# Value products of an encoder trunk: three matmuls of 256 columns replaced by one of 512 and one of 256

## Chip, cores and metric

The kernel runs on one core of a Trainium2 chip. The metric is the device time of one execution in microseconds (us), lower is better. Three runs of the kernel before took 2064.1, 2063.9 and 2063.29 us.

## What is computed

The reference is a trunk of two layers on 256 tokens of width 2048, all in float32. Each layer is a normalization, a projection to queries, keys and values, attention of 16 heads of width 128, an output projection with a residual, and an MLP of width 8192 with a squared ReLU. The part that the change touches is the projection to values.

```python
proj = h @ w_in                                            # layer 0: q, k, v of 16 heads
qa, ka, va, qb, kb, vb = jnp.split(proj, [...], axis=-1)
oa = neighbourhood_attention(split_heads(qa, 8), split_heads(ka, 8), split_heads(va, 8), rpb)
ob = dilated_attention(split_heads(qb, 8), split_heads(kb, 8), split_heads(vb, 8))
x = x + jnp.concatenate([merge_heads(oa), merge_heads(ob)], axis=-1) @ w_out
...
proj = h @ w_qkv                                           # layer 1: q of 16 heads, k and v of 4
q, k, v = jnp.split(proj, [wq, wq + wkv], axis=-1)
o = banded_attention(split_heads(q, 16), split_heads(k, 4), split_heads(v, 4), 128, 1, slopes, sink=sink)
x = x + merge_heads(o) @ w_out
...
x = x + sq_relu_mlp(rms_norm(x, g), w1, w2)                # after either attention
```

## The kernel before

**Precision.** A float32 product is made of three products of a rounded type (fp32r). Every operand is split in a high part (a copy in that type) and a low part (what the copy lost): `split` does it with one instruction on ACT (the high part, L86) and one on DVE (the low part, L87). The product is then high·high + high·low + low·high.

**Units.** A unit is a block of 128 columns of a weight matrix with all 2048 rows: 16 tiles of 128x128, which come in two halves of 8 tiles (512 KB each) by a DMA that SP issues. `load_halves` gives a half a raw buffer, a buffer for its high parts (`whi`, five of them) and one for its low parts (`wlo`, five). `k_range` multiplies: for each of 16 `k` there is a matmul of 512 columns (L160: the weight's high part is stationary, the activation's high and low parts lie side by side in `u` and move), and one of 256 columns (L162: the weight's low part by the activation's high part). The first fills a whole PSUM bank `acc` of 512 columns, the second adds to its first half. `joined` then copies the second half of the bank to SBUF on ACT (L189, tile `t`) and adds the first half to it on DVE (L191, tile `z`). There are three `acc` banks.

**Values.** The values of two heads (256 columns of weights) are needed with tokens on the partitions, so here the activation is stationary and the weights move. `value_products` (L281) does for each `k` and each half `j` of the tokens three matmuls of 256 columns: activation high by weight high, high by low, and low by high. All add to the same 256 columns of one bank, in which `j` = 0 and `j` = 1 lie side by side. There are 10 such pairs of heads: the first is in the start stage (L467 on, 16 packs that hold a slice of the input and of the first weights), seven more are in layer 0, two in layer 1. That is 10 x 16 x 2 x 3 = 960 matmuls. `keep_values` then reads the bank: ACT writes the high part `v` with the token's scale (L301), DVE the low part (L302).

**Order.** The code is written as one stream of units with steps that fall due after so many `tick`s (one per four `k` of a unit, or per two `k` of a value pair); a scheduler then orders each engine's instructions by what it expects to be ready. So where a step falls on an engine is not to be read from the code alone. Around the end of a value pair in layer 0 there stand: the first matmuls of the next unit, the transposes `p_ps` of the pair's second head (L342), and the products `m_ps` of the weights of attention with the values of the pair's first head (L361), which need `v`. Each `v` tile is read by six such matmuls a head: `v` high of `j` = 0 twice, then `v` low of `j` = 0, then the same for `j` = 1. Other names in the rows: `s_ps` are scores (L317), `st` and `s` the softmax, `pt` the transposed attention weights, `ssq` sums of squares, `rcol` the scale of a token, `toep` and `tabs` tables for the biases, `hid` the hidden part of the MLP, `o` the heads' outputs. L481 and L482 are the start stage's own products for the first two heads' queries and keys.

## Time and profile before

| | |
|---|---|
| median of three runs | 2063.9 us (2063.29 to 2064.1) |
| the profiled execution | 2064.23 us |
| its span, first to last instruction | 2062.3 us |
| granted TensorE clock, mean | 0.996 |
| PE busy (matmuls) | 2042.2 us, 99% |
| DVE busy, ACT busy | 1340.3 us (65%), 1036.9 us (50%) |
| instructions on PE | 12438 matmuls, 12438 loads of weights |

PE is the engine of the matmuls, PEld its loads of stationary operands, which run beside them. A matmul's own duration in the rows is from its start to its end with the pipeline's fill, so that durations overlap: a matmul of 512 columns shows 390 ns where the next one starts 227 ns later. What counts is the distance from one start to the next.

### The profile page before, as it was taken

The page shows a single profiled execution, that of the slowest core. Times are in us where ns is not written, and L with a number is a line of the kernel's source. Part 1 is how long each engine was busy: PE and PEld are TensorE (multiplying, and loading weights), DVE is VectorE, ACT ScalarE, POOL GpSimd, SP SyncE. Part 2 cuts the span into 40 slices and gives each one's busy share as a digit, 9 for nine tenths or more (in the row PEclk, how much of TensorE's full clock was granted, in tenths as well). Part 3 has the DMA queues.
Part 4 walks back from the last instruction along what each step waited for, and adds up shares of the span by engine and source line. Part 5 has one row for each costly group of instructions (what it writes and reads, how often), then busy time and mean ns, then how long its engine had stood idle before and what let it go on. Part 6 is the DMA issues. An engine that isn't in the chain of part 4 may idle for free.

```text
span 2062.3 us, 31803 instructions
## 1 busy us (share of the span) xinstructions
PE 2042.2 (99%) x12438; PEld 1825.3 (89%) x12438; DVE 1340.3 (65%) x2083; ACT 1036.9 (50%) x1597; POOL 18.5 (1%) x26
## 2 busy tenths in 40 slices
PE   8999999999999999999999999999999999999997
PEld 7999998888888888888889998888888888888886
DVE  7766666766655556666666877766665556665554
ACT  6555555554544444444445655654444444444442
POOL 2100000000000000000000000000000000000000
PEclk9999999999999999999999999999999999999998
DMA  8655555555555555555555444555555555555552
GB/s 311 204 174 168 175 169 184 195 186 193 194 194 194 193 194 195 194 194 194 194 194 185 154 155 152 189 188 193 195 193 192 194 195 193 193 193 194 193 193 92
DMA packets 107174, 388.16 MB, mean 188 GB/s; under 512 B 12128, under 2 KB 12400, under 8 KB 107024
## 3 DMA queue, kind: packets, MB, share of 16 engines
q1 hardware_dynamic: 106128, 383.83, 55.9%
q0 software_dynamic: 752, 2.27, 0.3%
q8 instruction: 97, 1.59, 0.3%
q14 instruction: 53, 0.43, 0.1%
q10 hardware_dynamic: 144, 0.04, 0.0%
HBM read 383.99 MB, written 2.10 MB: 187 GB/s over the span
## 4 chain that ended last, share of the span: by engine, by line
PE 98%; DVE 1%; DMA 0%; ACT 0%; issue 0%; POOL 0%; DVEq 0%; POOLq 0%
PE acc L160 58%; PE acc L162 30%; PE acc L281 5%; PE s_ps L317 1%; PE m_ps L361 1%; PE p_ps L342 1%; DMA tabs<-in_tabs 0%; PE s_ps L481 0%; PE acc L481 0%; ACT h L86 0%; DVE l L87 0%; DVE xs L581 0%; PE acc L482 0%; PE acc L158 0%; PE acc L157 0%
## 5 line engine op out<-in xcount | busy, mean ns | idle before, releaser
L87 DVE TENSOR_TENSOR l<-r,h 128x1024 fp32r<-128x1024 f32 (+1 forms) x724 | 881.3, 1217 | 654.2 <-ACT h L86 652.5
L86 ACT ACTIVATE h<-r 128x1024 fp32r<-128x1024 f32 (+1 forms) x724 | 762.4, 1053 | 915.5 <-PE acc L160 604.0
L160 PE MATMUL acc<-u,h 128*128 128x512 f32 x2804 | 960.5, 390 | 0.3 <-DVE z L191 0.3
L162 PE MATMUL acc<-u,l 128*128 128x256 f32 x2804 | 774.5, 276 | 0.0
L160 PE MATMUL acc<-hid,h 128*128 128x512 f32 x2016 | 685.6, 389 | 0.0
L160 PEld LDWEIGHTS acc<-u,h 128*128 128x128 f32 x2804 | 526.5, 188 | 107.1 <-DVE z L191 0.4
L162 PE MATMUL acc<-hid,l 128*128 128x256 f32 x2048 | 565.5, 276 | 0.0
L162 PEld LDWEIGHTS acc<-u,l 128*128 128x128 f32 x2804 | 526.5, 188 | 0.1
L160 PEld LDWEIGHTS acc<-hid,h 128*128 128x128 f32 x2016 | 378.4, 188 | 78.5
L162 PEld LDWEIGHTS acc<-hid,l 128*128 128x128 f32 x2048 | 384.5, 188 | 0.0
L160 PE MATMUL acc<-o,h 128*128 128x512 f32 x500 | 173.2, 392 | 1.2 <-DVE z L191 1.2
L162 PE MATMUL acc<-o,l 128*128 128x256 f32 x500 | 139.0, 278 | 0.0
L281 PE MATMUL acc<-h,u 128*128 128x256 f32 x640 | 122.2, 283 | 0.0
L191 DVE TENSOR_TENSOR z<-acc,t 128x256 f32<-128x256 f32 x273 | 113.6, 418 | 2.1 <-ACT t L189 2.1
L160 PEld LDWEIGHTS acc<-o,h 128*128 128x128 f32 x500 | 93.9, 188 | 21.9 <-DVE z L191 1.9
L281 PEld LDWEIGHTS acc<-h,u 128*128 128x128 f32 x640 | 101.7, 189 | 1.0
L189 ACT ACTIVATE t<-acc 128x256 f32<-128x256 f32 x273 | 100.2, 368 | 4.3 <-PE acc L162 2.3
L162 PEld LDWEIGHTS acc<-o,l 128*128 128x128 f32 x500 | 93.9, 188 | 0.0
L281 PE MATMUL acc<-l,u 128*128 128x256 f32 x320 | 90.3, 282 | 0.0
L281 PEld LDWEIGHTS acc<-l,u 128*128 128x128 f32 x320 | 60.6, 189 | 0.0
L403 DVE SCALAR_TENSOR_TENSOR z<-z 128x256 f32<-128x256 f32 x128 | 54.3, 425 | 4.2
L86 ACT ACTIVATE hid<-z 128x256 fp32r<-128x256 f32 x128 | 51.3, 402 | 6.0 <-DVE z L403 6.0
(105 smaller groups left out, 869.8 us busy)
## 6 DMA issues: line engine op xcount, KB each, us to landing
r<-in_w_mlp_in SPq DMA_DIRECT2D x256, 512.0 KB, 3.5
r<-in_w_mlp_out SPq DMA_DIRECT2D x256, 512.0 KB, 3.6
r<-in_even_w_in SPq DMA_DIRECT2D x56, 512.0 KB, 3.6
r<-in_odd_w_qkv SPq DMA_DIRECT2D x40, 512.0 KB, 3.5
r<-in_even_w_out SPq DMA_DIRECT2D x32, 512.0 KB, 3.5
r<-in_odd_w_out SPq DMA_DIRECT2D x32, 512.0 KB, 3.6
r<-in_even_w_v SPq DMA_DIRECT2D x28, 512.0 KB, 3.5
r<-in_start SPq DMA_DIRECT2D x16, 512.0 KB, 4.7
```

What stands on the lines that cost most here:

```text
L86: nc.scalar.activation(hi, src, AF.Copy)
L87: nc.vector.tensor_sub(lo, src, hi.bitcast(F32))
L160: nc.tensor.matmul(ps, h, act[:, k].rearrange("p a t -> p (a t)"), start=start, stop=False)
L162: nc.tensor.matmul(ps[:, :T], l, act[:, k, 0, :], start=False, stop=stop)
L189: nc.scalar.activation(t, ps[:, T:], AF.Copy)
L191: nc.vector.tensor_add(z, ps[:, :T], t)
L281: nc.tensor.matmul(out, u[:, k, x, js], y, start=k == 0 and j == 0 and n == 0, stop=k == KT - 1 and n == 2, skip_group_check=True)
L317: nc.tensor.matmul(s_ps[:, i, :], qh[:, x, qs], kh[:, y, :], start=n == 0, stop=n == 2)
L342: nc.tensor.transpose(p_ps[:, j, i * P:(i + 1) * P], s[:, i, j * P:(j + 1) * P], ident)
L361: nc.tensor.matmul(o_ps[:, :T], vv[:, x, j, side * P:(side + 1) * P], pt[:, y, j, :], start=n == 0, stop=n == 5)
L403: nc.vector.scalar_tensor_tensor(z, z, 0.0, z, op0=ALU.max, op1=ALU.mult)
```

## The change

The value products get the form of the other units. For each `k` and `j` there is one matmul of 512 columns (activation high by the weights' low and high parts side by side) and one of 256 (activation low by the weights' high part), which adds to the second half. Each `j` has a bank of its own, which is joined (ACT, DVE) before `keep_values` splits it: in the pairs after the first these are two of the three `acc` banks, in the start stage one `acc` and one `m_ps` bank. High and low parts of a half now lie in one buffer (five of 2112 columns, in place of five of 1024 and five of 1088), and for the values the low part stands first. In the start stage the weights of a pack, split in one step of 768 columns before, are split in two steps of 512 and 256.

```diff
+STEP = 16
+PART_SIZE = 2 * HALF * P + 4 * STEP
...
-    whi = ctx.enter_context(tc.tile_pool(name="whi", bufs=PART_BUFS))
-    wlo = ctx.enter_context(tc.tile_pool(name="wlo", bufs=PART_BUFS))
+    parts_w = ctx.enter_context(tc.tile_pool(name="parts_w", bufs=PART_BUFS))
...
+    def value_rows(w, n):
+        at = n * P + STEP
+        return w[:, STEP:STEP + 2 * at].rearrange("p (a c) -> p a c", c=at)[:, :, :n * P] \
+                .rearrange("p a (k c) -> p a k c", c=T)
...
             if flat:
-                h, l = (w.rearrange("p k c -> p (k c)") for w in (h, l))
-                split(h, l, r.rearrange("p k c -> p (k c)"))
-                loaded.append((h, l, None))
+                w = value_rows(w, HALF)
+                split(w[:, 1], w[:, 0], r.rearrange("p (k a) c -> p k (a c)", a=2))
+                loaded.append((w, None, None))
...
-    def value_products(ps, k, h, l):
+    def value_products(ps, k, w):
         for j in range(2):
             js = slice(j * P, (j + 1) * P)
-            out = ps[:, j * T:(j + 1) * T].rearrange("p (a c) -> p a c", a=2)
-            for n, (x, y) in enumerate(((0, h), (0, l), (1, h))):
-                nc.tensor.matmul(out, u[:, k, x, js], y, start=k == 0 and j == 0 and n == 0,
-                                 stop=k == KT - 1 and n == 2, skip_group_check=True)
+            nc.tensor.matmul(ps[j].rearrange("p (a t) -> p a t", a=2), u[:, k, 0, js], w, start=k == 0, stop=False)
+            nc.tensor.matmul(ps[j][:, T:], u[:, k, 1, js], w[:, 1, :], start=False, stop=k == KT - 1)
 
     def value_pair(pool, keep):
-        ps = acc_ps.tile([P, 2 * T], F32, name="acc")
+        ps = [acc_ps.tile([P, 2 * T], F32, name="acc") for _ in range(2)]
...
     def keep_values(pool, keep, ps):
-        ps = ps.rearrange("p (a t) -> p a t", a=2)
         w = pool.tile([P, 2, 2, T], F32R, name="v", bufs=1)
         for j in range(2):
-            nc.scalar.activation(w[:, 0, j, :], ps[:, j, :], AF.Copy, scale=rcol[:, j:j + 1])
-            nc.vector.scalar_tensor_tensor(w[:, 1, j, :], ps[:, j, :], rcol[:, j:j + 1],
+            z = joined(ps[j])
+            nc.scalar.activation(w[:, 0, j, :], z, AF.Copy, scale=rcol[:, j:j + 1])
+            nc.vector.scalar_tensor_tensor(w[:, 1, j, :], z, rcol[:, j:j + 1],
                                            w[:, 0, j, :].bitcast(F32), op0=ALU.mult, op1=ALU.subtract)
...
-    vps = acc_ps.tile([P, 2 * T], F32, name="acc")
+    vps = acc_ps.tile([P, 2 * T], F32, name="acc"), aux_ps.tile([P, 512], F32, name="m_ps", bufs=2)
...
-        h, l = (w[:, :6, :] for w in part_rows(HALF))
-        split(h, l, r[:, 2:, :])
+        w = parts_w.tile([P, PART_SIZE], F32R, name="w")
+        (h, l), v = part_rows(w, 4), value_rows(w[:, 8 * P + 4 * STEP:], 2)
+        split(h, l, r[:, 2:6, :])
+        split(v[:, 1], v[:, 0], r[:, 6:, :].rearrange("p (k a) c -> p k (a c)", a=2))
```

The scheduler orders the engines anew. Three places are shown.

PE after the end of the second value pair of layer 0's loop (the pairs that follow have the same order). Before, behind four `k` of the next unit, which are its first eight matmuls (the last two stand on top here):

```order
L160 MATMUL acc<-u,h 128x512
L162 MATMUL acc<-u,l 128x256
L342 MATMUL p_ps<-ident,s 128x128 x4
L361 MATMUL m_ps<-pt,v 128x256 x5
L160 MATMUL acc<-u,h 128x512
L162 MATMUL acc<-u,l 128x256
L160 MATMUL acc<-u,h 128x512
L162 MATMUL acc<-u,l 128x256
L160 MATMUL acc<-u,h 128x512
L361 MATMUL m_ps<-pt,v 128x256
```

After, at the same place (L167 and L169 are the unit's matmuls, L345 the transposes, L364 the products with the values):

```order
L167 MATMUL acc<-u,w 128x512
L169 MATMUL acc<-u,w 128x256
L345 MATMUL p_ps<-ident,s 128x128 x4
L364 MATMUL m_ps<-pt,v 128x256 x2
L167 MATMUL acc<-u,w 128x512
L169 MATMUL acc<-u,w 128x256
L167 MATMUL acc<-u,w 128x512
L169 MATMUL acc<-u,w 128x256
L167 MATMUL acc<-u,w 128x512
L169 MATMUL acc<-u,w 128x256
L364 MATMUL m_ps<-pt,v 128x256 x4
```

Of the six products with the values, five stood directly behind the transposes before and the last one five matmuls later; now two stand there and four come six matmuls later.

DVE at the same place. Before:

```order
L87 TENSOR_TENSOR l<-r,h 128x1024
L302 SCALAR_TENSOR_TENSOR v<-acc,rcol,v 128x256
L87 TENSOR_TENSOR l<-r,h 128x1024
L302 SCALAR_TENSOR_TENSOR v<-acc,rcol,v 128x256
L87 TENSOR_TENSOR pt<-p_ps,pt 128x512
```

After (L198 joins, L88 makes the low parts of weights, L305 those of `v`):

```order
L88 TENSOR_TENSOR w<-r,w 128x1024
L198 TENSOR_TENSOR z<-acc,t 128x256 x2
L88 TENSOR_TENSOR w<-r,w 128x1024
L305 SCALAR_TENSOR_TENSOR v<-z,rcol,v 128x256 x2
L88 TENSOR_TENSOR pt<-p_ps,pt 128x512
```

The two joins have come in ahead, and the low part of the next half's weights now stands ahead of both low parts of `v`. ACT goes through the same sequence: two copies `t`, a high part of weights, the two high parts of `v`, then `pt`.

DVE in the start stage, from its first split on. Before:

```order
L87 TENSOR_TENSOR l<-r,h 128x768
L203 SCALAR_TENSOR_TENSOR u<-r,g,u 128x256
L390 SCALAR_TENSOR_TENSOR toep<-tabs 128x384
L87 TENSOR_TENSOR l<-r,h 128x768
L214 TENSOR_TENSOR ssq<-ssq,sq 128x256
```

After:

```order
L88 TENSOR_TENSOR w<-r,w 128x512
L88 TENSOR_TENSOR w<-r,w 128x256
L210 SCALAR_TENSOR_TENSOR u<-r,g,u 128x256
L393 SCALAR_TENSOR_TENSOR toep<-tabs 128x384
L88 TENSOR_TENSOR w<-r,w 128x512
L88 TENSOR_TENSOR w<-r,w 128x256
L221 TENSOR_TENSOR ssq<-ssq,sq 128x256
```

Each split has become two; the step that waits for the tables (`toep`) stands where it stood.

## Rows read from the trace of the kernel before

**Rows 1.** The page's first and fourth part: busy time of PE and its loads, and the chain of work that ended last, by engine and by line.

```profile
PE 2042.2 (99%) x12438; PEld 1825.3 (89%) x12438; DVE 1340.3 (65%) x2083; ACT 1036.9 (50%) x1597; POOL 18.5 (1%) x26
...
PE 98%; DVE 1%; DMA 0%; ACT 0%; issue 0%; POOL 0%; DVEq 0%; POOLq 0%
PE acc L160 58%; PE acc L162 30%; PE acc L281 5%; PE s_ps L317 1%; PE m_ps L361 1%; PE p_ps L342 1%; DMA tabs<-in_tabs 0%; PE s_ps L481 0%; PE acc L481 0%; ACT h L86 0%; DVE l L87 0%; DVE xs L581 0%; PE acc L482 0%; PE acc L158 0%; PE acc L157 0%
```

**Rows 2.** The page's fifth part: the value products' matmuls with high weights moving, two thirds of them: count, busy time, mean ns of one.

```profile
L281 PE MATMUL acc<-h,u 128*128 128x256 f32 x640 | 122.2, 283 | 0.0
```

**Rows 3.** The chain that ended last, in order of time: the value products of two pairs of layer 0 (start, us on the chain, count).

```profile
111.58 1.42 PE acc L281 x12
113.43 5.73 PE acc L281 x48
...
119.88 4.24 PE acc L281 x36
...
148.62 1.42 PE acc L281 x12
150.48 5.66 PE acc L281 x48
156.85 4.24 PE acc L281 x36
```

**Rows 4.** Busy time by engine in the four long stretches that hold units alone: the MLP of layer 0, the output projection of layer 1 with what follows up to the next norm, the MLP of layer 1 (its last unit has three matmuls for each `k`), and the output projection of layer 0. The first column is the stretch and its length; the count behind PE is of matmuls, half of 512 and half of 256 columns; behind POOL stands the granted clock.

```profile
418.00:1107.00 689.00, 689.00 (x4054) 610.14 (x4054) 429.07 (x571) 325.40 (x443) 0.00 (x0) 1.00 0.58 194
1277.40:1363.60 86.20, 86.20 (x492) 75.55 (x493) 60.94 (x98) 49.54 (x83) 0.00 (x0) 1.00 0.56 183
1369.30:2045.00 675.70, 675.70 (x3998) 599.26 (x3997) 410.66 (x539) 316.69 (x429) 0.00 (x0) 1.00 0.56 187
328.80:412.00 83.20, 83.20 (x492) 73.56 (x491) 60.23 (x96) 49.18 (x81) 0.00 (x0) 1.00 0.58 190
```

**Rows 5.** The timeline of PE in the last unit, the only one of the other units that is made of matmuls of 256 columns alone (three for each `k`, weights stationary): one matmul, and the ninth behind it.

```profile
2045.07 0.28 PE L162 MATMUL acc<-hid,l 128*128 128x256 f32 x1
...
2046.12 0.28 PE L162 MATMUL acc<-hid,l 128*128 128x256 f32 x1
```

**Rows 6.** The timeline of PE at the end of the value pair that ended at 123.96 us.

```profile
123.96 0.39 PE L160 MATMUL acc<-u,h 128*128 128x512 f32 x1
...
125.68 0.84 PE L361 MATMUL m_ps<-pt,v 128*128 128x256 f32 x5
...
127.04 0.39 PE L160 MATMUL acc<-u,h 128*128 128x512 f32 x1
127.29 0.38 PE L361 MATMUL m_ps<-pt,v 128*128 128x256 f32 x1
127.51 0.28 PE L162 MATMUL acc<-u,l 128*128 128x256 f32 x1
```

**Rows 7.** The timeline of ACT at the same place; in brackets the idle time ahead and what ended it.

```profile
124.16 0.48 ACT L301 ACTIVATE v<-acc,rcol 128x256 fp32r<-128x256 f32 x1 [1.59 <-PE acc L281]
124.53 1.05 ACT L86 ACTIVATE h<-r 128x1024 fp32r<-128x1024 f32 x1
125.48 0.46 ACT L301 ACTIVATE v<-acc,rcol 128x256 fp32r<-128x256 f32 x1
```

**Rows 8.** The timeline of DVE at the same place.

```profile
124.67 0.48 DVE L302 SCALAR_TENSOR_TENSOR v<-acc,rcol,v 128x256 fp32r<-128x256 f32 x1 [0.84 <-ACT v L301]
125.61 1.23 DVE L87 TENSOR_TENSOR l<-r,h 128x1024 fp32r<-128x1024 f32 x1 [0.46 <-ACT h L86]
126.75 0.48 DVE L302 SCALAR_TENSOR_TENSOR v<-acc,rcol,v 128x256 fp32r<-128x256 f32 x1
```

**Rows 9.** Who waited for whom, for the loads of PE: us in total, times, longest.

```profile
PEld m_ps L361 <- DVE v L302: 1.0, 6, 0.2
```

**Rows 10.** Groups of instructions by line and form: count, busy time, mean ns of one. The join's two steps; a step of ACT and one of DVE that scale a tile of 256 columns in SBUF by a value for each partition, as `keep_values` will; a DVE subtraction of 512 columns.

```profile
L191 DVE TENSOR_TENSOR z<-acc,t 128x256 f32<-128x256 f32 x273 | 113.6, 418 | 2.1 <-ACT t L189 2.1
L189 ACT ACTIVATE t<-acc 128x256 f32<-128x256 f32 x273 | 100.2, 368 | 4.3 <-PE acc L162 2.3 <-DVE z L191 1.8
...
L202 ACT ACTIVATE u<-xs,g 128x256 fp32r<-128x256 f32 x48 | 23.8, 496 | 0.5 <-DVE xs L376 0.4
...
L203 DVE SCALAR_TENSOR_TENSOR u<-xs,g,u 128x256 fp32r<-128x256 f32 x48 | 23.0, 480 | 0.0
L87 DVE TENSOR_TENSOR pt<-p_ps,pt 128x512 fp32r<-128x512 f32 x32 | 21.8, 682 | 0.2 <-ACT pt L86 0.2
```

**Rows 11.** The timeline of all engines in the start stage.

```profile
12.34 0.56 DVE L390 SCALAR_TENSOR_TENSOR toep<-tabs 128x384 f32<-128x384 f32 x1 [5.30 <-DMA tabs<-in_tabs]
12.81 0.95 DVE L87 TENSOR_TENSOR l<-r,h 128x768 fp32r<-128x768 f32 x1
...
13.82 0.80 PE L482 MATMUL acc<-u,l 128*128 128x256 f32 x2 [5.06 <-DVE l L87]
...
14.41 0.95 DVE L87 TENSOR_TENSOR l<-r,h 128x768 fp32r<-128x768 f32 x1
```

**Rows 12.** The timeline of PE in the start stage: the first matmul of two packs that follow each other.

```profile
42.21 0.39 PE L481 MATMUL acc<-u,h 128*128 128x512 f32 x1
...
44.28 0.39 PE L481 MATMUL acc<-u,h 128*128 128x512 f32 x1
```

**Rows 13.** Busy time by engine behind the start stage, where the first heads' queries, keys and values are split; columns as in rows 4 (PE, PEld, DVE, ACT).

```profile
52.30:61.00 8.70, 8.65 (x53) 7.48 (x52) 8.25 (x22) 6.26 (x17) 0.31 (x1) 1.00 0.84 282
```

More of the change, by code (lines that the diff above doesn't have):

```diff
@@ L27 @@
 HALF = KT // 2
-LO_AT = 16
+STEP = 16
+PART_SIZE = 2 * HALF * P + 4 * STEP
 RAW_BUFS = 6
@@ L118, in load_halves @@
             if n < HALF:
-                h, l = part_rows(2, held_w, held_w, "h")
+                h, l = part_rows(held_w.tile([P, 4 * P + 4 * STEP], F32R, name="hw"), 2)
                 split(h, l, r[:, n:, :])
@@ L273, in head_parts @@
         return done
-    def value_products(ps, k, h, l):
+    def value_products(ps, k, w):
         for j in range(2):
             js = slice(j * P, (j + 1) * P)
-            out = ps[:, j * T:(j + 1) * T].rearrange("p (a c) -> p a c", a=2)
-            for n, (x, y) in enumerate(((0, h), (0, l), (1, h))):
-                nc.tensor.matmul(out, u[:, k, x, js], y, start=k == 0 and j == 0 and n == 0,
-                                 stop=k == KT - 1 and n == 2, skip_group_check=True)
+            nc.tensor.matmul(ps[j].rearrange("p (a t) -> p a t", a=2), u[:, k, 0, js], w, start=k == 0, stop=False)
+            nc.tensor.matmul(ps[j][:, T:], u[:, k, 1, js], w[:, 1, :], start=False, stop=k == KT - 1)
     def value_pair(pool, keep):
-        ps = acc_ps.tile([P, 2 * T], F32, name="acc")
+        ps = [acc_ps.tile([P, 2 * T], F32, name="acc") for _ in range(2)]
         for half in range(2):
-            parts = [take_half()[:2] for _ in range(2)]
+            parts = [take_half()[0] for _ in range(2)]
             for kk in range(HALF):
-                h, l = (w[:, (kk % 4) * T:(kk % 4 + 1) * T].rearrange("p (a c) -> p a c", a=2)
-                        for w in parts[kk // 4])
-                value_products(ps, half * HALF + kk, h, l)
+                value_products(ps, half * HALF + kk, parts[kk // 4][:, :, kk % 4, :])
                 if kk % 2 == 1:
```

12 lines of the change are left out of this document (6 added, 6 removed).

## Prediction

> **What bounds the kernel now.** I read the page's busy times and chain first [rows 1]: the chain is PE for 98% of the span, and the reader is to see that no other engine or transfer holds more than 1%. So a saving counts only if it shortens the distance from one matmul's start to the next, and any wait put before PE counts in full. The value products (L281) hold 5% of the chain; their matmuls show 283 ns each [rows 2], but that includes the pipeline's fill, so I take distances. On the chain 96 matmuls of a pair take 1.42 + 5.73 + 4.24 = 11.39 us, those of the next pair 1.42 + 5.66 + 4.24 = 11.32 us [rows 3]: 118.6 and 117.9 ns, mean 118.3 ns for 256 columns. Then I looked at what the other units pay for the form that the values get. In the MLP of layer 0, 4054 matmuls take 689.0 us, 170.0 ns each, so a pair of 512 and 256 columns takes 339.9 ns. In a second stretch, with the same pairs, 492 take 86.2 us, 350.4 ns a pair [rows 4]. The same 768 columns thus run at two paces, 340 and 350. Nothing waits in either; the granted clock is 1.00 (2.4 GHz) in both.
>
> **Term 1, the matmuls: -4.8 us.** Three matmuls cost 3 x 118.3 = 354.9 ns, the pair that replaces them 339.9, so 15.0 ns less, 10 x 16 x 2 = 320 times: 4.8 us. The columns are the same 768; what goes is one matmul in three, with its load of weights. That the number of matmuls is the cause, and not what the value products read, is supported by the last unit: it has weights stationary and three matmuls of 256 columns, and nine of them take 1.05 us, 116.7 ns each [rows 5], nearly the value products' pace. At the slower pace of the second stretch the gain is 354.9 - 350.4 = 4.5 ns, 1.4 us in all; if the values keep their own rate per column (354.9 / 768), it is nothing. I take 4.8 because the pairs before and behind a value pair run at 340.
>
> **Term 2, the start stage: -0.3 us.** PE resumes at 13.82 after 5.06 us, as soon as DVE has made a low part of 768 columns (12.81, 0.95 us), which in turn stood behind `toep`, waiting for its table [rows 11]. The queries' and keys' part is now 512 columns, 0.68 us [rows 10], so PE resumes about 0.27 us earlier; the table comes when it came. The extra step costs ACT and DVE nothing on the path: DVE needs 1.60 us a pack (12.81 to 14.41), at most 0.68 + 0.42 - 0.95 = 0.15 more now, while PE takes 2.07 us a pack [rows 11, 12]. Bounds: -0.5 and, if the first packs go out of step, +0.2.
>
> **Term 3, the joins behind a pair: +1.2 us.** Ten pairs add 20 copies on ACT (368 ns) and 20 additions on DVE (418) [rows 10]. Neither engine holds the chain, but they make `v` later, and PE comes for `v` 1.7 us after a pair's end. Before: the pair ends at 123.96, the products with `v` start at 125.68 and the last one, which waits for the second low part (DVE from 126.75 to 127.23), starts at 127.29 instead of 127.27, and the next matmul 0.22 instead of 0.12 later: about 0.13 us lost a pair [rows 6, 8]; the list of waits has the same wait, 6 times 0.2 us [rows 9]. After, counted from the pair's end: the first `v` on ACT began at 0.20 before [rows 7], and now the second copy `t` can; a 1024-column split follows at 0.47, and since ACT takes the next step 0.95 us behind such a split (124.53 to 125.48), `v` of `j` = 0 runs from 1.42 to 1.92 (0.50 us [rows 10]). PE wants it at 1.72, so it loses 0.2 us. Three unit pairs later, at 3.2 us, it wants the low part: on DVE the weights' low part can start when ACT has made the high one, 1.55, the next step comes 1.14 behind (125.61 to 126.75 [rows 8]) at 2.69 and ends at 3.17; that is just in time, with 0 to 0.1 lost. So 0.2 to 0.4 us a pair against 0.13, about 0.17 more, in the seven later pairs of layer 0: 1.2 us. In the first pair and in layer 1 whole units lie between. Bounds: 0, and 0.65 a pair (4.5 us) if both halves come late by half a weight split.
>
> **Term 4, behind the start stage: +0.2 us.** Between 52.3 and 61.0 DVE is busy 8.25 of 8.70 us and PE 8.65 [rows 13]. Two additions, 0.84 us, come in, and the first `v` must wait for a `z` buffer, since four are held by queries and keys. 0.45 us fits in the gaps; the rest can delay scores that PE wants. PE has whole units to do meanwhile, so I take 0.2, bounds 0 and 0.8.
>
> **Edits at nothing.** One buffer for both parts makes the next split wait for the 256-column matmul behind the 512 one, 0.11 us; the ring holds five halves, over 10 us of work, and ACT idles half of the time [rows 1]. Two `acc` banks for a pair: the third holds the unit before, and both others were joined a unit (5.4 us) ago, so PE does not wait; were a join late, PE would, with all that is queued behind. In layer 1's first pair the second bank is still being joined, and the order there puts four `k` of `j` = 0 ahead. DMAs are the same in number, size and order.
>
> **Sum.** -4.8 - 0.3 + 1.2 + 0.2 = -3.7 us. Against the profiled execution (2064.23, a span of 2062.3 and 1.9 around it) that is 2060.5; this execution lay 0.3 above the median 2063.9, and for the median I say 2060.2. A measurement of this kernel tells about 0.2% from no change, 4.1 us, so the forecast is just inside "same".
>
> **Rivals.**
>
> *B, a slow stretch goes too: 2057.6.* The 246 pairs from 1277.4 on run at 350 [rows 4]. They begin when PE restarts after a wait; how it restarts seems to set the pace until the next interruption. The change shifts what lies ahead of it. If the restart falls to 340, 246 x 10.5 ns = 2.6 us more goes. Against it: the last 30 us ahead of that wait have the same work in the same order.
>
> *C, the number of matmuls is not the cause: 2064.2.* If the value products are slow for what they read (weights moving from the split's buffers), 512 columns take 237 ns and the pair 355, term 1 is nothing, and the rest is left: +1.1, or -0.3 at the 350 pace; in the middle 2064.2. Rows 5 speak against it. A rule comes out near this: the Trainium skill, page "TensorE: Matmul & The Clock Gate", section "Back-to-back issue gap", gives a warm matmul its columns over 2.4 GHz and 2.5 ns, 109.2 ns for 256 columns and 215.8 for 512. By it three cost 327.6 and the pair 325.0, the 320 groups save 0.8 us, and the sum is +0.3. The traces show 118.3 ns for the one and 339.9 for the pair, so they do not agree with it.
>
> *D, a long stretch falls to the slow pace: slower, 2081.* The mechanism is that of B, with the other sign. The MLP of layer 0 is 2027 pairs at 340 [rows 4], entered after a norm's matmul interrupts PE; at 350.4 it would cost 2027 x 10.5 ns = 21 us. It decides from about 350 pairs on (3.7 us). Two MLPs stand at risk. For it: the pace does change at restarts. Against it: only one long stretch of four is slow [rows 4].
>
> *E, the joins cost what the matmuls give: 2063.4.* With term 3 at its upper bound the sum is -0.4.
>
> **How the numbers follow.** A (the forecast) 0.50, B 0.20, C 0.13, E 0.09, D 0.08. The forecast's own range is 2058.7 to 2062.2. A lies below 2059.8 (faster by over 0.2%) with 0.18 of its 0.50; with B that makes 0.38 for faster. Same: 0.32 + 0.13 + 0.09 = 0.54. Slower: 0.08. The range from 2056.4 to 2064.9 takes in A, B, E and C with its bounds, and leaves out D and the tails.
>
> **What would show it.** Term 1: on the chain a pair's 64 matmuls take 32 x 0.340 = 10.9 us instead of 11.35; at C they take 11.35. Term 2: PE's first long wait ends near 13.5. Term 3: the list of waits shows loads of L364 waiting for ACT's and DVE's `v`, 0.2 to 0.4 us a pair. Term 4: PE's busy time from 52 to 61. B and D: matmul counts over time in the MLPs and from 1277 on. A wait of PE for an `acc` bank at a pair, or a pace of 350 in an MLP, would make the prediction wrong.

## The result, and the profile of the changed kernel

| | before | changed |
|---|---|---|
| median, us (16 runs each) | 2063.75 | 2067.11 |
| lowest to highest | 2061.46 to 2065.16 | 2064.28 to 2068.03 |
| profiled execution, its span | 2064.23, 2062.3 | 2067.98, 2065.5 |

Ratio 1.0015, interval 1.0008 to 1.0022: slower by some 3 us, where 2060.2 (2056.4 to 2064.9) was forecast. The runs of the changed kernel stand in two groups, four at 2064.3 to 2065.4 and twelve at 2066.4 to 2068.0.

Page, first and fourth part, of the changed kernel [rows 1]:

```profile
PE 2045.5 (99%) x12118; PEld 1812.1 (88%) x12118; DVE 1359.1 (66%) x2119; ACT 1058.0 (51%) x1633; POOL 18.5 (1%) x26
...
PE 96%; DVE 1%; ACT 1%; DMA 1%; issue 0%; POOL 0%; DVEq 0%; ACTq 0%; POOLq 0%
```

There are 320 matmuls fewer, as the change says, and PE is busy 3.3 us longer. On the chain ACT's and DMA's 1% are new. So the loss must be sought in the distances between matmuls. I compared when the same matmul starts in the two traces, place by place (changed minus before, us):

| place | before, us | later by |
|---|---|---|
| first matmul of the norm behind the start stage | 46.38 | +0.59 |
| 2nd value pair of layer 0's loop, first matmul | 111.42 | +0.82 |
| ... its end (first matmul of the next unit) | 123.96 | +0.57 |
| 7th value pair, first matmul | 296.58 | +1.04 |
| ... its end | 309.20 | +0.88 |
| norm behind the projection of layer 0 | 412.77 | +3.79 |
| norm behind the projection of layer 1 | 1364.30 | +3.78 |
| last norm | 2048.36 | +3.78 |

Two things are to be seen. From the second pair's start to the seventh's, each pair gains (0.14 to 0.25) and each stretch behind a pair loses about as much (0.15 to 0.27). And nearly the whole of the 3.2 us by which the span grew, 2.9, appears in one place that has no value products: between the 7th pair and the norm behind the projection of layer 0. The windows of the four long unit stretches say what happened there [rows 4]:

```profile
422.00:1107.00 685.00, 685.00 (x4032) 606.48 (x4031) 430.01 (x568) 328.79 (x440) 0.00 (x0) 1.00 0.59 193
1281.40:1367.20 85.80, 85.80 (x491) 75.19 (x491) 61.11 (x97) 50.28 (x82) 0.00 (x0) 1.00 0.56 184
1373.00:2045.00 672.00, 672.00 (x3966) 595.55 (x3965) 414.03 (x537) 322.06 (x430) 0.00 (x0) 1.00 0.57 188
329.90:415.70 85.80, 85.80 (x491) 75.19 (x491) 61.10 (x97) 50.28 (x82) 0.00 (x0) 1.00 0.56 185
```

Before, 492 matmuls of the last stretch took 83.2 us (338 ns a pair); now 491 take 85.8 (349.5). It runs at the slow one of the two paces, as the projection of layer 1 (now from 1281 on) did before and does still. In the starts of the matmuls, 246 pairs in a row, to the next norm, are 350 ns apart where they were 340: 246 x 10.5 ns = 2.6 us. The rest of the 2.9 is the stretch behind the 7th pair and a wait ahead of the projection that is 0.11 us longer. The granted clock is 1.00 in all four.

**The value pairs.** Chain in order of time, eight pairs of 512 and 256 columns of the second value pair [rows 3]:

```profile
117.01 0.23 PE acc L286
...
119.80 0.70 PE s_ps L320 x6
```

2.79 us for eight is 349 ns each, where 340 was forecast and three matmuls had taken 354.9. The median over all value pairs is 349 in this trace.

**Behind a pair.** Timeline of PE, ACT and DVE behind the second pair [rows 6 to 8], three fences:

```profile
124.53 0.39 PE L167 MATMUL acc<-u,w 128*128 128x512 f32 x1
...
125.90 0.60 PE L345 MATMUL p_ps<-ident,s 128*128 128x128 f32 x4
126.56 0.51 PE L364 MATMUL m_ps<-pt,v 128*128 128x256 f32 x2
126.91 0.39 PE L167 MATMUL acc<-u,w 128*128 128x512 f32 x1
...
127.93 0.68 PE L364 MATMUL m_ps<-pt,v 128*128 128x256 f32 x4
```

```profile
124.36 0.81 ACT L196 ACTIVATE t<-acc 128x256 f32<-128x256 f32 x2 [1.14 <-PE acc L287]
125.06 1.05 ACT L87 ACTIVATE w<-r 128x1024 fp32r<-128x1024 f32 x1
126.01 0.90 ACT L304 ACTIVATE v<-z,rcol 128x256 fp32r<-128x256 f32 x2
```

```profile
124.78 0.85 DVE L198 TENSOR_TENSOR z<-acc,t 128x256 f32<-128x256 f32 x2 [0.30 <-ACT t L196]
126.15 1.23 DVE L88 TENSOR_TENSOR w<-r,w 128x1024 fp32r<-128x1024 f32 x1 [0.52 <-ACT w L87]
127.29 0.88 DVE L305 SCALAR_TENSOR_TENSOR v<-z,rcol,v 128x256 fp32r<-128x256 f32 x2
```

ACT makes both copies `t` before the weight split, and `v` only behind it, from 126.01; PE's products with `v` start at 126.56, 2.03 us after the pair's end (1.92 was forecast), and the next unit matmul at 126.91. From the transposes (125.90, four at 0.11) to there it is 0.57 us more than they take, for two products of about 0.12. The second group, at 127.93, is hardly late. The list of waits says the same [rows 9]: the wait for DVE's `v` has become one for ACT's, and is twice as long. The last two rows are the waits of PE and its loads for a first join (behind the start stage and in the two output projections); PE's was 1.5 us in all before:

```profile
PEld m_ps L364 <- ACT v L304: 2.1, 7, 0.3
PEld acc L167 <- DVE z L198: 2.5, 3, 1.1
PE acc L167 <- DVE z L198: 1.8, 3, 0.8
```

**The start.** PE resumes at 13.75 (before 13.82 [rows 11]); `toep` came 0.2 us later:

```profile
12.54 0.56 DVE L393 SCALAR_TENSOR_TENSOR toep<-tabs 128x384 f32<-128x384 f32 x1 [5.22 <-DMA tabs<-in_tabs]
...
13.75 0.80 PE L487 MATMUL acc<-u,w 128*128 128x256 f32 x2 [4.68 <-DVE w L88]
```

But the granted clock, at 0.50 behind the wait, comes back at different times: windows of 2 us of the changed kernel, then of the kernel before. Each is one execution.

```profile
14.00:16.00 2.00, 2.00 (x8) 1.81 (x9) 2.00 (x7) 1.59 (x4) 0.62 (x1) 0.50 0.98 308
16.00:18.00 2.00, 2.00 (x8) 1.71 (x7) 2.00 (x6) 1.95 (x6) 2.00 (x2) 0.50 0.90 240
18.00:20.00 2.00, 2.00 (x8) 1.67 (x8) 2.00 (x2) 1.38 (x4) 1.74 (x2) 0.54 0.67 266
```

```profile
16.00:18.00 2.00, 2.00 (x10) 1.79 (x10) 2.00 (x4) 1.95 (x5) 1.93 (x1) 0.61 0.94 258
18.00:20.00 2.00, 2.00 (x15) 1.87 (x14) 2.00 (x2) 0.89 (x2) 1.33 (x2) 1.00 0.88 326
```

### The profile page after: what moved, and what is told of

It reads as the page before. It is cut to its first block, busy times and chain, and to the rows that moved or that the text cites. A ratio compares the mean times of both kernels' runs of the same rounds, so it can differ in the third digit from the quotient of the medians.

```text
span 2065.5 us, 31226 instructions
## 1 busy us (share of the span) xinstructions
PE 2045.5 (99%) x12118; PEld 1812.1 (88%) x12118; DVE 1359.1 (66%) x2119; ACT 1058.0 (51%) x1633; POOL 18.5 (1%) x26
## 4 chain that ended last, share of the span: by engine, by line
PE 96%; DVE 1%; ACT 1%; DMA 1%; issue 0%; POOL 0%; DVEq 0%; ACTq 0%; POOLq 0%
PE acc L167 57%; PE acc L169 29%; PE acc L286 3%; PE acc L287 2%; PE m_ps L364 1%; PE s_ps L320 1%; ACT w L87 1%; DVE w L88 1%; PE p_ps L345 0%; DMA tabs<-in_tabs 0%; PE s_ps L486 0%; PE acc L486 0%; ACT t L196 0%; DVE xs L586 0%; PE acc L487 0%
## 5 line engine op out<-in xcount | busy, mean ns | idle before, releaser
L88 DVE TENSOR_TENSOR w<-r,w 128x1024 fp32r<-128x1024 f32 (+1 forms) x740 | 881.2, 1193 | 531.8 <-ACT w L87 523.0
L87 ACT ACTIVATE w<-r 128x1024 fp32r<-128x1024 f32 (+1 forms) x740 | 761.6, 1032 | 629.9 <-PE acc L169 523.9
L167 PE MATMUL acc<-u,w 128*128 128x512 f32 x2804 | 960.4, 390 | 0.3 <-DVE z L198 0.3
L169 PE MATMUL acc<-u,w 128*128 128x256 f32 x2804 | 775.1, 276 | 0.0
L167 PE MATMUL acc<-hid,w 128*128 128x512 f32 x2016 | 685.6, 389 | 0.0
L167 PEld LDWEIGHTS acc<-u,w 128*128 128x128 f32 x2804 | 526.6, 188 | 107.8 <-DVE z L198 0.4
L169 PE MATMUL acc<-hid,w 128*128 128x256 f32 x2048 | 565.5, 276 | 0.0
L169 PEld LDWEIGHTS acc<-u,w 128*128 128x128 f32 x2804 | 526.5, 188 | 0.1
L167 PEld LDWEIGHTS acc<-hid,w 128*128 128x128 f32 x2016 | 378.4, 188 | 78.5
L169 PEld LDWEIGHTS acc<-hid,w 128*128 128x128 f32 x2048 | 384.5, 188 | 0.0
L198 DVE TENSOR_TENSOR z<-acc,t 128x256 f32<-128x256 f32 x292 | 122.7, 422 | 116.6 <-ACT t L196 116.3
L167 PE MATMUL acc<-o,w 128*128 128x512 f32 x500 | 175.4, 395 | 1.5 <-DVE z L198 1.5
L169 PE MATMUL acc<-o,w 128*128 128x256 f32 x500 | 140.0, 280 | 0.0
L167 PEld LDWEIGHTS acc<-o,w 128*128 128x128 f32 x500 | 94.0, 188 | 23.0 <-DVE z L198 2.1
L169 PEld LDWEIGHTS acc<-o,w 128*128 128x128 f32 x500 | 93.9, 188 | 0.0
```

Source lines behind the costliest of these rows:

```text
L87: nc.scalar.activation(hi, src, AF.Copy)
L88: nc.vector.tensor_sub(lo, src, hi.bitcast(F32))
L167: nc.tensor.matmul(ps, h, act[:, k].rearrange("p a t -> p (a t)"), start=start, stop=False)
L169: nc.tensor.matmul(ps[:, :T], l, act[:, k, 0, :], start=False, stop=stop)
L198: nc.vector.tensor_add(z, ps[:, :T], t)
```

## The experiments

**Theory**: the loss is the projection of layer 0 at 350 ns a pair, taken over when TensorE starts again behind a wait; the value form itself is worth about nothing, because it gives 0.2 us a pair and takes it back in the wait for `v`. **Rivals**: the pace follows from where the weights now lie; the loss lies in the value form or in the start. Each kernel is compared with runs of the kernel before on the same chip, medians 2064.08 to 2064.47; there are 10 or 11 runs of each, seven of `a_late_nowait`, five of `a_best`. The last two rows are one run each, of kernels that compute another product, and are read for their paces alone. The paces are those of the profiled execution. TensorE is the engine that the rows call PE.

| kernel | projection of layer 0, of layer 1, ns a pair | median, us (lowest to highest) |
|---|---|---|
| before | 340, 350 | 2064.2 (2061.4 to 2064.9), first batch |
| a_again | 350, 350 | 2067.0 (2065.5 to 2069.5) |
| b_kick | 340, 350 | 2064.3 (2060.9 to 2065.6) |
| a_kick | 350, 350 | 2066.9 (2066.1 to 2068.8) |
| a_kick2 | 350, 340 | 2065.5 (2064.4 to 2068.3) |
| a_kick3 | 350 then 340, twice | 2065.8 (2064.7 to 2068.0) |
| a_hifirst | 350, 340 | 2067.3 (2064.7 to 2069.0) |
| a_contig | 350, 340 | 2067.3 (2063.7 to 2068.9) |
| b_onebuf | 340, 350 | 2064.9 (2061.4 to 2068.0) |
| a_four | 350, 350 | 2063.7 (2062.0 to 2068.3) |
| a_fill | 350, 340 | 2063.7 (2060.8 to 2066.7) |
| a_late_o | 340, 350 | 2063.1 (2060.6 to 2066.0) |
| a_laterz | 340, 340 | 2063.2 (2062.1 to 2065.1) |
| b_nowait | 340, 340 | 2059.9 (2059.4 to 2061.0) |
| a_nowait | 340, 340 | 2060.7 (2059.9 to 2062.1) |
| a_late_nowait | 340, 340 | 2058.4 (2058.0 to 2060.0) |
| a_best | 340, 340 | 2057.5 (2056.7 to 2057.7) |
| a_statw | 350, 350 | 2067.5, one run |
| a_movu | 350, 340 | 2065.9, one run |

### The changed kernel again: a_again

No edit.

> The changed kernel once more, unaltered, as the control for the others. Theory 'pace': most of its loss is the output projection of layer 0 (330 to 416 us), which ran at 350 ns a pair in its profile and at 340 in that of the kernel before; the change made that the usual state, so the profile shows 350 there again (246 pairs, 2.6 us) and the time is 1.0010 to 1.0020 of the kernel before. Rival 'work': the pace of that stretch is a matter of the single execution, in both kernels alike, and the loss is the work of the change (joins, waits for v, the start); then the stretch may well run at 340 here with the ratio still at 1.0015.

2067.0, ratio 1.0017 (1.0008 to 1.0026). Again both projections at 350. At the first norm it was 1.0 us ahead of the kernel before, not 0.6 behind: the start differs from execution to execution by more than the change moves it.

### Two small matmuls in the row: b_kick, a_kick, a_kick2, a_kick3

In `project_out`, for `b_kick` and `a_kick` with `c == 3`, for `a_kick2` with `c == 5`:

```
+            if c == 3:
+                kp = aux_ps.tile([P, 512], F32, name="m_ps", bufs=2)
+                for j in range(2):
+                    nc.tensor.matmul(kp[:, j:j + 1], ones, ones[:, 0:1], start=True, stop=True)
             unit(done(c), o)
```

> The kernel before, with two more matmuls of 128 columns to 1 in each output projection, ahead of its fourth unit (of the kind that the norm issues at 1364 us, behind which the slow stretch of layer 1 ended). Their sums go nowhere. If an interruption of this kind resets the pace, the stretch of layer 1 runs at 340 from there on: 212 pairs x 10.5 ns = 2.2 us less, two interruptions of 0.4 us more, so 1.4 us less in an execution that had the slow stretch, ratio near 0.9993. If the pace belongs to the stretch (its operands or addresses), it stays at 350 and the time rises by 0.8 us, ratio 1.0004.

> The changed kernel with the same two interruptions. 'Pace': both projections run at 340 behind them, 2 x 2.2 us less and 0.8 more, 3.6 us below the changed kernel, ratio 0.9997 to the kernel before. 'Work', or a pace that belongs to the stretch: 0.8 us above the changed kernel, ratio 1.0019.

> The changed kernel with two matmuls of one column put between the fifth and the sixth unit of each projection, behind the point at which TensorE has started again. Theory 'the pace of a long stretch is set when TensorE starts and held until something else stands in the row': the stretches from 329 and 1281 us go over to 340 ns behind the two matmuls, 2 x 2.1 us less, plus 2 x 0.4 for the matmuls, 2063.5. Rival 'the pace belongs to the stretch (addresses, neighbours), not to its start': 350 ns on both sides of the two matmuls, 2067 to 2068.

All three missed what they were made for. The small matmuls depend on nothing, so they were put into TensorE's wait, ahead of the restart (at 328.37 in `a_kick2`, restart 329.24). They say only that a small matmul in the wait itself doesn't fix the pace: `a_kick` stayed at 350 twice, `b_kick` at 340 and 350 as before. Where they read the residual of unit 6, they came where they were wanted:

```
             unit(done(c), o)
+            if c == 8:
+                kp = aux_ps.tile([P, 512], F32, name="m_ps", bufs=2)
+                for j in range(2):
+                    nc.tensor.matmul(kp[:, j:j + 1], ones, xs[:, 6, j:j + 1], start=True, stop=True)
```

> The changed kernel with two matmuls of one column that read the residual of unit 6, so that they come in the middle of each projection's long stretch. Theory 'a stretch holds the pace that it started with until something else stands in TensorE's row': the slow stretches go over to 340 ns (or take a new pace) behind the two matmuls, some 150 pairs x 10 ns = 1.5 us each, less 0.4 us for the matmuls: 2065 to 2066. Rival 'the pace is held over them': 246 pairs at 350 ns, 2067.0 to 2068.

2065.8, 1.2 below the changed kernel. Windows ahead of the two matmuls (361.67 and 1312.14) and behind them, in both projections:

```profile
328.90:361.00 32.10, 32.10 (x186) 28.07 (x185) 23.42 (x39) 18.95 (x32) 0.00 (x0) 1.00 0.50 170
362.40:414.00 51.60, 51.60 (x307) 45.65 (x305) 37.12 (x58) 30.97 (x51) 0.00 (x0) 1.00 0.60 197
1279.50:1311.40 31.90, 31.90 (x184) 27.91 (x183) 23.25 (x38) 18.82 (x32) 0.00 (x0) 1.00 0.51 170
1312.80:1364.50 51.70, 51.70 (x307) 45.73 (x305) 37.20 (x58) 31.11 (x51) 0.00 (x0) 1.00 0.60 195
```

186 matmuls in 32.1 us are 345 ns a pair (edges counted in), 307 in 51.6 are 336; in the starts, 94 pairs in a row are 350 apart ahead of the two matmuls, and 340 behind them, in both layers. The part behind them ran at 350 in the changed kernel. So the pace is held from the restart until something else stands in the row, and it is no property of the weights, the addresses or the neighbours of that stretch.

### No wait at the start of the stretch: a_nowait, b_nowait

```
-    def unit(done, act, srcs=1, summed=False):
-        ps = acc_ps.tile([P, 2 * T], F32, name="acc")
+    def unit(done, act, srcs=1, summed=False, ps=None):
+        if ps is None:
+            ps = acc_ps.tile([P, 2 * T], F32, name="acc")
...
+            ps = None
+            if c == 3:
+                ps = aux_ps.tile([P, 2, T], F32, name="s_ps", bufs=2).rearrange("p a t -> p (a t)")
+            unit(done(c), o, ps=ps)
```

> The changed kernel with one thing else: the fourth unit of each projection adds up in a bank that the scores have left, so that TensorE doesn't stand for the first join there (0.98 and 1.03 us in the trace of the changed kernel). Theory 'the pace of 350 ns of these stretches is taken at the start after that wait and held to the next norm': both stretches run at 340 ns, 2 x 2.6 us less, with the waits 2.0 less: 2059.8 to 2060.5. Rival 'the pace belongs to the stretch': both stay at 350 ns and only the waits go, 2065.0 to 2065.4.

> The kernel before with the same bank for the fourth unit of each projection (waits of 0.87 and 0.92 us there). Theory 'the pace is taken at the start after the wait': no stretch at 350 ns, 2064.2 - 2.6 - 1.7 = 2059.9, and no executions 2.5 us apart from each other any more. Rival 'the pace belongs to the stretch': 2062.4. If both this kernel and the changed one with the bank are free of the slow pace, their difference is what the value form itself is worth: by the trace of the changed kernel 0 to 0.5 us less for it (1.7 won in the pairs, 1.8 lost behind them).

2060.7 and 2059.9, both faster than the kernel before (ratios 0.9982, 0.9973 to 0.9991, and 0.9980, 0.9971 to 0.9989). Windows of both projections, `a_nowait`, then `b_nowait`:

```profile
328.80:412.00 83.20, 83.20 (x491) 73.61 (x490) 61.67 (x99) 50.41 (x82) 0.00 (x0) 1.00 0.57 193
1277.40:1360.00 82.60, 82.60 (x488) 73.05 (x487) 61.11 (x97) 50.40 (x82) 0.00 (x0) 1.00 0.55 191
```

```profile
328.80:412.00 83.20, 83.20 (x491) 73.58 (x491) 61.10 (x98) 49.55 (x83) 0.00 (x0) 1.00 0.54 192
1277.40:1360.00 82.60, 82.60 (x488) 73.06 (x487) 60.58 (x97) 49.20 (x82) 0.00 (x0) 1.00 0.54 192
```

All four stretches run at 339 ns a pair. From 2067.1, two stretches (5.2) and the waits (1.5 by PE's list) give 2060.4; 2060.7 was measured. The runs also draw together: over 2.2 and 1.6 us, where those of the changed kernel spread over 3.8. What is left between the two kernels is the value form itself: 0.8 us **more** for the changed one by the medians, in lists that overlap. I had expected 0 to 0.5 less.

### One buffer alone: b_onebuf

```
-        h = hi_pool.tile([P, n, P], F32R, name=tag + "h")
-        l = lo_pool.tile([P, n * P + 64], F32R, name=tag + "l")
-        return h, l[:, LO_AT:LO_AT + n * P].rearrange("p (k c) -> p k c", c=P)
+        w = pool.tile([P, 2 * n * P + 64], F32R, name=tag + "w")
+        at = n * P + LO_AT
+        return (x.rearrange("p (k c) -> p k c", c=P) for x in (w[:, :n * P], w[:, at:at + n * P]))
```

> The kernel before with one thing of the change: high and low part of a weight tile lie in one buffer (low part 64 bytes behind the high one), values as before in three matmuls of 256 columns and kept straight from the accumulator. Theory 'the pace of the projection of layer 0 follows from where the weights lie': the stretch of units from 328 us falls to the 350 ns pace here too, about 2066.5 us (before 2064.2 plus 2.6 less noise). Theory 'it follows from what the value form does to the time at which TensorE starts again': that stretch stays at 340 ns as before, 2064.2 within 0.5. The value pairs of matmuls stay at 354 to 355 ns for 96 matmuls' third in both.

Between the two: median 2064.9, ratio 1.0006 (0.9997 to 1.0015), the profiled execution with 340 and 350 as before. But four of 11 runs lie at 2066.8 to 2068.0, where none of the kernel before on that chip is above 2065.4. So one buffer makes that height possible in some runs; whether it is the projection of layer 0 at 350 in those four was not seen, since only one execution is profiled. PE's wait there is longer with one buffer, as in the changed kernel (from the last matmul to the restart 0.98 us, before 0.87).

### A later restart: a_laterz

```
+        if extra:
+            nc.vector.tensor_copy(z[:, :extra], t[:, :extra])
         nc.vector.tensor_add(z, ps[:, :T], t)
...
-                z = joined(ps)
+                z = joined(ps, 128 if c == 0 else 0)
```

> The changed kernel with one small copy of 128 columns on VectorE ahead of the first join of each projection, so that TensorE starts again some 0.1 to 0.2 us later. Theory 'the moment of the start decides the pace': the stretch of layer 0, slow in seven of the profiled runs of the changed kernel and its relatives that were not moved before it, comes out at 340 ns in a part of the runs, and the runs stand 2.6 us apart: lowest ones at 2062 to 2064. Rival 'it is slow whenever the change is there': 2067.3 to 2067.5, the added wait on top.

2063.2, some 3.8 us **faster** than the changed kernel for a wait that is 0.14 us longer in each layer. Timeline of PE at the restart of layer 0, changed kernel, then `a_laterz`, and windows of `a_laterz`:

```profile
328.67 0.28 PE L169 MATMUL acc<-o,hw 128*128 128x256 f32 x1
329.65 0.50 PE L167 MATMUL acc<-o,w 128*128 128x512 f32 x1 [0.70 <-DVE z L198]
```

```profile
328.27 0.28 PE L169 MATMUL acc<-o,hw 128*128 128x256 f32 x1
329.38 0.50 PE L167 MATMUL acc<-o,w 128*128 128x512 f32 x1 [0.84 <-DVE z L200]
```

```profile
330.00:415.00 85.00, 85.00 (x504) 75.20 (x503) 61.98 (x98) 51.77 (x84) 0.00 (x0) 1.00 0.58 190
1279.00:1364.00 85.00, 85.00 (x503) 75.25 (x502) 62.22 (x99) 51.69 (x85) 0.00 (x0) 1.00 0.57 190
```

504 matmuls in 85.0 us: 337 ns a pair, no 350 in either. Ten of 11 runs lie between 2062.1 and 2063.8, below the lowest of the changed kernel. On the same chip `a_kick3`, with the restart as in the changed kernel, has no run below 2064.7. So with the restart 0.14 us later the runs stand where two fast stretches put them.

The length of the wait does not tell which pace comes, though. Ahead of the projection of layer 0 the traces have the same wait as in the changed kernel, 0.98 us to within 2 ns, in front of 350 nine times and in front of 340 twice (`b_onebuf`, `a_late_o`); ahead of that of layer 1, 1.03 us to within 4 ns, it is 350 seven times and 340 four times. `a_late_o` and `a_four` came down to 2063 with these waits as they were, so a later restart is one way to the fast pace and not the only one. What does tell the two apart is the first pair behind the restart, from its first matmul to the next of 512 columns: in all 32 such restarts of the profiled executions that wait in a projection it takes 454 to 456 ns where the row goes on at 350 (21 times), and 451 to 453 or 459 to 464 where it goes on at 340 (11 times). So the pace goes with a shift of some nanoseconds within that first pair; behind the start stage 454 is followed by 340 as well, so this is a sign and no rule.

### Products with v later: a_late_o, a_late_nowait

```
-            if not v or now[0] < state["at"] + lags[2]:
+            if not v or now[0] < max(state["at"] + lags[2], made.get(id(v), (v, -9))[1] + 2):
```

(`made` holds the step at which a pair was kept.)

> The changed kernel with one thing else: the products with v of the head that stands behind a pair of value units come two steps later (some 8 matmuls pairs of the next unit in front of them), so that TensorE no longer stands for the high part of v. Theory 'the wait for v costs 0.23 to 0.3 us in each of 7 stretches behind a pair': 1.6 to 2.1 us less than the changed kernel, 2065.0 to 2065.4. Rival 'the time behind a pair goes to other things (bank, reads of softmax)': within 0.5 of 2067.0.

> The changed kernel with both: products with v two steps later, and the bank for the fourth unit. Theory 'wait for v and pace are the whole loss, and they add': 2063.1 for the first alone, its lowest executions without a slow stretch 2061, less 2.0 for the two waits: 2058.5 to 2059.5, that is 4.7 to 5.7 under the kernel before, and 1.5 to 2 under the changed kernel with the bank alone. Rival 'the wait for v shrinks by itself when TensorE runs evenly': within 0.5 of the changed kernel with the bank alone.

2063.1, some 4 us below the changed kernel. No row for PE or its loads waiting for `v` is left in the list of waits, and behind the second pair the six products stand together and flow:

```profile
126.46 0.28 PE L169 MATMUL acc<-u,w 128*128 128x256 f32 x1
126.57 0.88 PE L367 MATMUL m_ps<-pt,v 128*128 128x256 f32 x6
127.29 0.40 PE L167 MATMUL acc<-u,w 128*128 128x512 f32 x1
```

From the start of one value pair to the next (mean of six) it is 37.04 us before, 37.08 changed, 36.73 here: 0.35 a pair. That makes some 2.5 us in seven; the rest may be the projection of layer 0, which ran at 340 in the profiled execution. With both edits, where no stretch is slow, the price stands alone: 2058.4 against 2060.7 of `a_nowait`, 2.3 us, somewhat over the 1.5 to 2 expected; the rival falls. Against `b_nowait` it is 1.6 less, so with `v` later the changed kernel is ahead; how much of that the kernel before would gain from a later `v` was not tried.

### The start: a_fill, and all three: a_best

```
+        if k == 0:
+            for _ in range(20):
+                nc.tensor.matmul(wps[:, :P], ones, ones, start=True, stop=True)
```

> The changed kernel with 20 matmuls of one tile more in the start, while TensorE waits 4.7 us for the first tables (they write a bank that nothing reads). Theory 'the clock at 0.50 behind that wait costs 1 to 2 us, and the 0.6 us that the changed kernel was behind at the first norm is when it comes back': clock at 1.00 from the first products on, 1.0 to 1.5 us less than the changed kernel, 2065.5 to 2066. Rival 'the start is set by the transfers of the packs, TensorE waits for them anyway': within 0.4 of 2067.0, or up to 1 us more for the matmuls.

> The changed kernel with the three things together: products with v two steps later, the bank for the fourth unit, 20 matmuls in the start's wait. If they add: 2058.4 for the first two, less 0.7 to 1.0 for the start, 2057.4 to 2057.7. If the start is bound by its packs behind the first norm anyway: 2058.4.

Windows of `a_fill`:

```profile
14.00:16.00 2.00, 2.00 (x13) 1.75 (x12) 2.00 (x6) 1.88 (x5) 0.57 (x2) 1.00 1.03 306
16.00:18.00 2.00, 2.00 (x13) 1.78 (x12) 2.00 (x5) 1.98 (x6) 2.00 (x1) 1.00 0.86 281
```

The clock is 1.00 from the restart on, and the first norm comes at 44.8 us against 45.4 to 47.0 in the changed kernel's two profiles. 2063.7 is 3.4 below the changed kernel, but 2.6 of that may be a projection at 340 (one of two in its trace), so the kernel alone is inconclusive on the price. `a_best`, where no stretch is slow, is 2057.5 against 2058.4 of `a_late_nowait`: 0.9 us by the medians, 0.5 when each is taken against the kernel before on its own chip (6.6 and 6.1 below it), at or just under what was expected. `a_best` is the fastest kernel of the study, 0.9969 of before (0.9956 to 0.9981).

### Why a value pair takes 349 ns: a_hifirst, a_contig, a_four, a_statw, a_movu

Five edits, one each (high part first, with the 256 columns added to the first half of the bank; both parts side by side without a gap; four `k` for one half of the tokens before the other; weights loaded in place of `u`; `u` streamed in place of weights):

```
+            nc.tensor.matmul(ps[j][:, :T], u[:, k, 1, js], w[:, 0, :], start=False, stop=k == KT - 1)
...
+        return w[:, STEP:STEP + 2 * n * P].rearrange("p (k a c) -> p a k c", a=2, c=T)
...
+            for i, w in enumerate(ws, k):
...
+            nc.tensor.matmul(ps[j].rearrange("p (a t) -> p a t", a=2), w[:, 0, js], w, start=k == 0, stop=False)
...
+            nc.tensor.matmul(ps[j], u[:, k, 0, js], u[:, k].rearrange("p a t -> p (a t)"), start=k == 0, stop=False)
```

> The changed kernel with the high part first: the matmul of 256 columns then adds to the first half of the bank, as in the other units, and no longer to the half that the matmul of 512 wrote last. In the profile after, a value pair of matmuls took 351 ns (235 + 116), not the 340 forecast. Theory 'same columns': a matmul that adds to the columns written just before it is slower; then the pair falls to 340 here, 320 x 11 ns = 3.5 us less than the changed kernel, ratio 0.9998. Rival 'operands' (weights from u, moving columns in two pieces): it stays at 348 to 352 and the time is that of the changed kernel, 1.0010 to 1.0020.

> The changed kernel with one thing else: low and high part of a value weight lie directly side by side, so the 512 moving columns are one piece instead of two. Theory 'the two pieces make the wide value matmul slower than that of a unit': a pair of 512 and 256 columns falls from 349 to 340 ns in the value pairs, 320 x 9 ns = 2.9 us, so 2064.2. Rival 'it is the load of the weights (u as stationary) or the pace that the stretch has': stays at 348 to 350 ns and 2067.0.

> The changed kernel with the value matmuls of a pair in groups of four k for one half of the tokens, then four for the other, so that the bank changes every eighth matmul and not every second. Theory 'the change of bank after every pair costs the 9 ns by which a value pair is slower than a unit pair': the median falls from 349 to 342 to 343 ns, 320 x 6.5 = 2 us less, 2065. Rival 'it is the stationary side (u loaded, weights moving)': 348 to 349 ns, 2067.0.

> The changed kernel with value products whose stationary side is a piece of the value weights in place of u (another product, so its output is not the reference's); columns and count as they are. Theory 'loading u as the stationary side costs the 9 ns': 340 to 342 ns a pair. Rival 'streaming weights as the moving side costs them': 349 ns.

> The changed kernel with value products of 512 columns that stream u in place of the value weights (another product, so its output is not the reference's); stationary side u, the 256-column matmul as it is. Theory 'streaming weights as the moving side costs the 9 ns': 340 to 343 ns a pair. Rival 'loading u as the stationary side costs them': 349 ns.

Median of a value pair in the traces: 350 in `a_hifirst`, 349 in `a_contig` and `a_four`, 347 in `a_statw` and `a_movu`. Neither the order of the parts, nor the two pieces, nor the change of bank, nor either operand alone brings it to 340. Every theory here fell, and the cause stays open; both operands at once were not exchanged. (`a_four` is at 2063.7 for another reason: its runs stand in two groups, seven at 2062.0 to 2064.0 and three at 2066.2 to 2068.3, of which the profiled one, 2067.0, has both projections at 350.)

## Why the prediction was wrong, point by point

**Term 1, the matmuls (-4.8).** The sign was right, the size not. The pair takes 349 ns, not the 339.9 of the units around it: 320 x (354.9 - 349) = 1.9 us, near the lower bound that I had given (1.4). "I take 4.8 because the pairs before and behind a value pair run at 340" was the step that failed: neighbours don't hand on their pace. Rival C (nothing gained, for what the value products read) was nearer in time; its cause is neither shown nor excluded, since either operand exchanged alone gave 2 of the 9 ns (`a_statw`, `a_movu`). By the Trainium skill's rule ("TensorE: Matmul & The Clock Gate", "Back-to-back issue gap"), which the section gives for the isolated gap of a single matmul, 325.0 ns is an estimate for the pair; no run here shows that, and three paces for the same 768 columns (340, 349, 350) are not in it.

**Term 2, the start (-0.3).** Not to be seen in the time. PE's wait ended at 13.75 and 13.44 in the changed kernel's two profiles, where 13.5 was forecast, but they are 0.6 behind and 1.0 ahead of the kernel before at the first norm. The term was smaller than the scatter of the clock's return, which `a_best` prices at 0.5 to 0.9 us.

**Term 3, the joins (+1.2).** The mechanism was as told, link by link: two copies on ACT, the weight split, then `v`, 2.03 us after the pair's end where 1.92 was forecast. Its price is 0.24 us a pair more than before (the stretches behind the pairs), 1.7 us in seven, and 0.35 a pair in all (`a_late_o`).

**Term 4, behind the start stage (+0.2).** From the first norm to the second pair's start the changed kernel loses 0.23, in one execution of each. The size is right, but it was luck as far as the trace tells: the sign that I had named, PE's busy time, is 8.65 of 8.70 us as before [rows 13] (the stretch is 0.6 us later now), and PE stands 0.05 us for the first scores' operands in both.

```profile
52.90:61.60 8.70, 8.65 (x53) 7.48 (x52) 8.55 (x23) 6.07 (x15) 0.00 (x0) 1.00 0.81 261
```

**Edits at nothing.** I had put at nothing that one buffer makes the next split wait for the 256-column matmul, 0.11 us, since the ring holds five halves and ACT idles half of the time. Ahead of an output projection it reaches TensorE: ACT's split there is released by the 256-column matmul (L169, and L161 in `b_onebuf`) and no longer by the 512-column one (L160). It starts 1.73 us ahead of TensorE's last matmul instead of 1.84, and DVE's split, the join and the restart come behind it. Timeline of ACT, kernel before, changed kernel, `b_onebuf`:

```profile
325.59 1.06 ACT L86 ACTIVATE h<-r 128x1024 fp32r<-128x1024 f32 x1 [0.98 <-PE acc L160]
```

```profile
326.94 1.06 ACT L87 ACTIVATE w<-r 128x1024 fp32r<-128x1024 f32 x1 [0.98 <-PE acc L169]
```

```profile
326.62 1.06 ACT L85 ACTIVATE w<-r 128x1024 fp32r<-128x1024 f32 x1 [0.98 <-PE acc L161]
```

This is the whole difference between a wait of 0.87 us and one of 0.98.

**The sum of these** with what was measured is -1.9 + 1.7 + 0.2 = 0.0, and `a_nowait` against `b_nowait` says +0.8. So with no slow stretch the forecast's own sum, -3.7, would still have been wrong by 4 us or so, mostly (2.9) by term 1.

**What then moved the time** is rival D's mechanism at rival B's kind of place. I had put it on the MLPs, at 21 us and a chance of 0.08, and had B only as a gain at the projection of layer 1, with "the last 30 us ahead of that wait have the same work in the same order" against it. That the other projection, which starts in the same way behind the same wait and ran at 340, could fall to 350, at 2.6 us, was in no rival. The row for it was there: [rows 4] show the two projections side by side, one at each pace. And order was the wrong thing to argue from: the moment of the restart matters, 0.14 us of it in `a_laterz`. The change moved that moment (from the last matmul to the restart 0.87 us before, 0.98 now); that this shift is what turned the stretch is not shown, since `b_onebuf` has it too and ran at 340 in its profiled execution. The account closes within 0.3: 0.8 for the form (from lists that overlap), 2.6 for one stretch and 0.2 for the longer waits make 3.6, and the medians differ by 3.4.

**Open.** What in the moment of a restart gives 340 or 350, and what makes the changed kernel's come out at 350 in layer 0; why a value pair takes 349; whether the kernel before would gain from a later `v` too (it waits 1.0 us for it [rows 9]; not tried).

## What to carry to other kernels

Where a long row of matmuls starts behind a short wait, look at the pace on both sides of it before costing anything else: a wait of 0.7 us cost 2.6 us more behind it, and a free bank for one unit removed both (with both projections 4.5 us on the kernel before, ratio 0.9980). A gain of some ns a matmul isn't read from a neighbour; it has to be read from a row of the same kind, or bounded by the slower pace. And where the value of an edit is below the step between two paces, take the steps out first, then compare.

## What the runs showed of the hardware

- The same row of fp32r matmuls (512 and 256 columns by turns) runs at 340 or at 350 ns a pair at a granted clock of 1.00 (2.4 GHz). The pace is taken at a restart behind a wait, within the first pair (454 to 456 ns ahead of 350 in the projections, fewer or more ahead of 340), kept over 246 pairs, and dropped at two matmuls of one column (`a_kick3`). The same wait, to within 2 ns, came out at either. Both parts stretch alike: in the starts 227 and 113 ns, or 233 and 117.
- A longer wait can make a kernel faster: 0.14 us more, 3.8 us less (`a_laterz`).
- Behind the wait in the start (4.7 us in the changed kernel) TensorE ran at 0.50 of its clock (1.2 GHz) for 3 to 6 us, differently in each execution; 20 matmuls in the wait keep it at 1.00 (2.4 GHz), worth 0.5 to 0.9 us (`a_best`).
